# C's projection in the output projection's banks, the third token form two weight units sooner, v scaled by quarters

## The chip, the cores and the metric

The kernel runs on one NeuronCore of a Trainium2 chip. The metric is the device time of one execution in microseconds, as the median of several. Its engines have a queue each and work in the order of their queues: TensorE (PE, with its weight loads as PEld), VectorE (DVE), ScalarE (ACT), GpSimd (POOL) and SyncE (SP, which issues most of the DMAs).

## What is computed

Two layers over 640 tokens (512 of a new stream and 8 x 16 of running streams) with 1024 channels, and a final norm. Layer A is a Mamba-2 mixer, layer B a gated MLP whose positions are mixed:

```python
# layer A, per group of 4 heads (8 groups)
xbc_c = silu(causal_dwconv(xbc, conv_prev, conv_w, conv_b))   # x (2 tiles of 128), B, C
y, ssm_new = ssd_scan(xs, dt, a, bm, cm, ssm_prev)            # C B^T, decay, states
y = gated_group_rms_norm(y + d_skip * xs, z, norm_w)
h = h + y @ w_out
# layer B
u = gelu(proj[..., :2048]); v = gelu(proj[..., 2048:4096]); z = proj[..., 4096:]
v = layer_norm(v, ln_w, ln_b)
s = einsum('gts,bksgc->bktgc', wm, vc) + b_sp                 # positions mixed, 8 groups
h = h + (u * s * silu(z)) @ w_out
```

All products run as three products of high and low parts (`hi*hi + lo*hi + hi*lo`), so weights and tokens are split into two tiles (`wh`, `wl` or `wf`, and `xH`, `xL`).

## The kernel before

**Layer A** goes through 8 groups. A group projects x0, x1, B, C, z0 and z1 (`in_proj`: two token halves of 384 and 256, 8 steps each, 16 in all; a step is three matmuls per 128 rows of weights). Work of other kinds is put between these steps: `side` is a list of closures, and `in_proj` takes one from it (`pump`) after each step named in `at`. `queue(j)` (L521) puts two closures there, which transpose the convolved tile j (0 and 1 are x0 and x1, 2 is B) to tokens: four tiles, then one (L472, tile `tp`, in ps_y). `conv_tile` reads a projection's two banks on VectorE (L415 to L417) and convolves it (L422, L425, L431, L432). After that a group runs its scan: `prompt_states` (tile `st` in ps_op, read by L569 into `hs`), `old_states` (`yq` in ps_op, read by L585), `cb_prompt` and `cb_sample` (ps_m), the masks (L634: the decays E of four heads times CBm, three on VectorE and one on GpSimd) and two pairs of heads (`yA`, `yB`, both in ps_y). In groups 1 to 6 the output projection of the group before is mixed in as ten pieces (`some`, L610): a piece is six matmuls into a bank named by the letter at its place in a string (o is ps_op, y is ps_y, m is ps_m), and is drained by L689 on VectorE. The order is: states 0, piece 0, old states, C B^T, piece 1, states 1, pieces 2 to 4, first mask, first pair, second mask, pieces 5 to 9, second pair.

PSUM has four pools of two banks: ps_in, ps_m, ps_y and ps_op. x0, x1, C, z0 and z1 are projected in ps_in, and B in ps_m. In layer A the order of TensorE is the order of the program; the order of the other engines and queues is set by Tile's scheduler, which works by priority and a model of its own.

**Layer B** has the order of all engines written by hand. First `v_tiles` makes v in four blocks of 512 columns (`vb`), tile by tile of 128 tokens (the last two tiles, 3 and 4, together), in four weight units u of 256 rows; after each unit it calls `unit(u)`. GELU is L844, the statistics L847. In the last block `unit` fills the first weight forms of the next stage: `forms.fill(2 * u + 2)`; a form is a 512-column combination of weight blocks, split by a cast on ScalarE (L751) and a subtraction on VectorE (L752), with L763, L765, L766 and L770 for the combinations. Forms of the tokens are made too: `t1_` to `t4_` between the tiles; the third, `t3`, is written over block (0, 1) of xH and xL by `hilo` (L905 on ScalarE, L906 on VectorE) after the last block, for that block is still read by the v matmuls. `t3` lies in a pool (`tfp`) that is closed there, and the tiles of the next stage (`wkb`: rsb, c1, uu, zz) take its memory.

Then 16 steps f (two per group g) compute u and z by seven products of 320 columns (Strassen-Winograd), in the order m1, m6, m5, m2, m7, m3, m4, in the banks pa, pb and pc. Between them stand c1 (L1015 reads pa), L1018 (reads pb), L1022 (reads pc), GELU (L1025, L1036), L1030, L1035 and L1049; m2 overwrites pa after L1015, m7 goes on in pb after L1018, m3 in pc after L1022, m4 in pb after L1030. `prod` first fills the weight forms five ahead. `v_norm(t)` (L850) scales v[:, t] to the layer norm: statistics and rsqrt on VectorE, then two activations of 1024 columns (L859); tiles 0 to 2 in the v stage, tiles 3 and 4 in step f = 0, behind L1025 and behind L1030. v's quarter f // 4 is read by the position mix of step f. Gating work of a step is put off into `later`, of which `then()` takes one entry between the products of the next step, and `then(9)` all that are left. In steps 3, 5, ..., 13 the ten output pieces of the group before come first, each drained by L968.

The lines that the change touches: L528 and L531 (the projections of B and C in groups 1 to 7), L610 (the banks of the pieces), L850 to L859 (`v_norm`), L946 and L947 (`unit` and `hilo`), L1027, L1032 and L1081 (`v_norm(3)`, `v_norm(4)` and `later`).

Of the kernel before, what the change touches and what calls it, by code (L numbers as in the profile page):

```python
# [8 lines left out]
F32 = mybir.dt.float32  # L9
F32R = mybir.dt.float32r  # L10
I32 = mybir.dt.int32
AF = mybir.ActivationFunctionType
# [3 lines left out]
P = 128  # L16
D = 1024
NT = 640
TT = 5
# [21 lines left out]
def hybrid_step(ctx: ExitStack, tc: tile.TileContext, xin, xT0, cst, wdt, cache, wA, wAo, h0in, wB, wBv, wBo,  # L41
                lnwb, spc, bsp, nwb, y_out, nconv_out, sspP_out, sspS_out, v_out):
    nc = tc.nc
    V, S, G, T = nc.vector, nc.scalar, nc.gpsimd, nc.tensor
# [217 lines left out]
    def in_proj(W, xT, pool=None, tag="in", at=(1, 3, 5, 7, 9, 11, 13)):  # L262
        outs = []
        for h, (a, b) in enumerate(HALVES):
            o = (pool or ps_in).tile([P, 512], F32, name="pin", tag=tag)[:, :b - a]
            outs.append(o)
            for k in range(KD):
                in_proj_step(W, xT, o, h, k)
                if 8 * h + k in at:
                    pump()  # L270
        return outs


    def out_proj(Ws, ys, acc, pieces=range(2 * TT), banks="oyoyoyoyoy", after=None, at=(1, 3)):
        for p in pieces:
            t, dh = p // 2, p % 2
            tsl = slice(t * P, (t + 1) * P)
            dsl = slice(dh * 512, (dh + 1) * 512)
            ps = bank(banks[p], "pop")
            n = len(ys)  # L280
            for i in range(n):
                (wH, wL), (yH, yL) = Ws[i], ys[i]
                mm(ps, yH[:, tsl], wH[:, dsl], start=(i == 0), stop=False)
                mm(ps, yL[:, tsl], wH[:, dsl], start=False, stop=False)
                mm(ps, yH[:, tsl], wL[:, dsl], start=False, stop=(i == n - 1))
            acc(ps, t, dsl)
            if after is not None:
                after(t, dsl, dh)
            if p in at:
                pump()  # L290
# [33 lines left out]
    with ExitStack() as ca:  # L324
# [123 lines left out]
        for g in range(GROUPS):  # L448
# [76 lines left out]

            if g:
                queue(0, *(() if g == 1 else (0,)))
                o = in_proj(stream.next(), xT, ps_m, "m", at=(3, 7, 11, 14))  # L528
                xcs.append(conv_tile(*o, 16 + g, 2, *cio))
                queue(1, *(() if g == 1 else (1,)))  # L530
                o = in_proj(stream.next(), xT, at=(3, 7, 11, 14))  # L531
                xcs.append(conv_tile(*o, 24 + g, 3, *cio))
                queue(2, *((0, 1, 2, 3) if g == 1 else (2, 3)))
            else:
                queue(0, 0)
                queue(1, 1)
                queue(2, 2, 3)
# [69 lines left out]
            ssd = [lambda: prompt_states(0), old_states, cb_prompt, lambda: prompt_states(1), cb_sample]  # L607
            if 0 < g < GROUPS - 1:
                Wo = [stream.next(), stream.next()]
                some = lambda a, b: out_proj(Wo, *pend[g - 1], range(a, b), "yyomoooyoo")  # L610
                ssd[0]()
                some(0, 1)
                ssd[1]()
                ssd[2]()
                some(1, 2)
                ssd[3]()
                ssd[4]()
                some(2, 5)
            elif last:
                side.extend(ssd)  # L620
                zrs.append(gate_in((1, 3, 5, 7, 9, 11, 13)))
                pump(9)
            else:
                side.extend(ssd)
                xin1 = in_proj(stream.next(), xT, at=(1, 3, 5, 8, 10))
                pump(9)
                cio1 = conv_io(1)
# [163 lines left out]
    with ExitStack() as cb_:  # L791
# [58 lines left out]
        def v_norm(t):  # L850
            mv = small.tile([P, 2], F32, name="mv")
            V.bn_aggr(out=mv, in_=st6[:, t])
            rs = rsqrt(mv[:, 1:2], EPS, 1)
            nm = small.tile([P, 1], F32, name="nm")
            V.scalar_tensor_tensor(nm, mv[:, 0:1], -1.0, rs, ALU.mult, ALU.mult)
            vt = v[:, t].rearrange("p a b -> p (a b)")
            for q in range(2):
                qs = slice(q * 1024, q * 1024 + 1024)
                S.activation(vt[:, qs], vt[:, qs], AF.Identity, scale=rs, bias=nm)  # L859

        def position(g):

# [32 lines left out]
        with tc.tile_pool(name="tfp", bufs=1) as tfp:  # L895
            ta, tb, t3, tx = [tfp.tile([P, 4, HT], F32, name=f"tx{i}") for i in range(4)]

            def sub(out, a, b):
                V.tensor_tensor(out=out, in0=a, in1=b, op=ALU.subtract)

            def add(out, a, b):
                V.tensor_tensor(out=out, in0=a, in1=b, op=ALU.add)

            def hilo(t, H, L):
                S.copy(out=H, in_=t)  # L905
                V.tensor_tensor(out=L, in0=t, in1=H.bitcast(F32), op=ALU.subtract)  # L906

            f11, f12, f21, f22 = [[x.bitcast(F32) for x in block(k, j)] for k in range(2) for j in range(2)]

            def t1_():  # L910
                sub(ta, f12[0], f11[0])
                sub(tx, f12[1], f11[1])
                add(ta, ta, tx)
                hilo(ta, tf[:, 0, 0], tf[:, 0, 1])

            def t2_():
                sub(tb, f22[0], ta)
                add(tb, tb, f22[1])
                hilo(tb, tf[:, 1, 0], tf[:, 1, 1])

            def t4_():
                sub(ta, f21[0], tb)
                add(ta, ta, f21[1])
                hilo(ta, tf[:, 2, 0], tf[:, 2, 1])

            def t3_():
                sub(t3, f22[0], f12[0])
                sub(tx, f22[1], f12[1])
                add(t3, t3, tx)

            between = {(1, 0): t1_, (1, 1): t2_, (2, 0): t4_, (2, 1): t3_}
            for vb in range(1, 4):
                W, vsp = vsp, []
                if vb < 3:
                    for u in range(4):
                        v_fetch(4 * vb + 4 + u)
                else:
                    forms.fetch()
                    forms.fetch()
                    pos = position(0)  # L940
                for t in range(3):
                    v_tiles(W, vb, (t,))
                    between.get((vb, t), lambda: None)()
                    if vb == 3:
                        v_norm(t)
                v_tiles(W, vb, (3, 4), unit=(lambda u: v_split()) if vb < 3 else (lambda u: forms.fill(2 * u + 2)))  # L946
            hilo(t3, *block(0, 1))  # L947
        wk = cb_.enter_context(tc.tile_pool(name="wkb", bufs=2))

        X = dict(m1=block(0, 0), m2=block(1, 0), m3=block(1, 1), m7=block(0, 1))  # L950
# [38 lines left out]
        for g in range(GROUPS):  # L989
# [9 lines left out]
            for i in range(2):  # L999
# [24 lines left out]
                prod(pa, "m2", False)  # L1024
                S.activation(uu[:, lo], pa, AF.Gelu)  # L1025
                if f == 0:
                    v_norm(3)  # L1027
                then()
                prod(pb, "m7", False)
                V.tensor_tensor(out=zz[:, hi], in0=pb, in1=c5, op=ALU.add)  # L1030
                if f == 0:
                    v_norm(4)  # L1032
                then(9)
                prod(pc, "m3", False)
                V.tensor_tensor(out=uu[:, hi], in0=pc, in1=uu[:, hi], op=ALU.add)  # L1035
# [42 lines left out]

                if f:
                    positions()  # L1080
                    later.extend([gate1, gate2, new_v])  # L1081
                else:
                    later.extend([gate1, lambda m=mix, p=positions: (m(), p()), gate2, new_v])

# [133 lines left out]
```

## Time and profile before

| | |
|---|---|
| median of 3 runs | 1084.14 us (1083.35 to 1085.52) |
| the profiled execution | 1084.73 us |
| its span, first to last instruction | 1083.0 us |
| mean granted TensorE clock | 0.983 |
| layer A | about 0 to 597 us |
| the v stage of layer B | about 597 to 718.6 us |
| the 16 steps and the end | 718.6 to 1083 us |

The profile is one execution. Starts and durations are in microseconds from the span's start. TensorE matmuls are pipelined, so their durations overlap. In brackets behind a row of the timeline stands how long the engine was idle before it, and what ended that.

### The profile page before, as it was taken

How to read it: one execution, taken by the hardware profiler on the slowest of the kernel's cores; microseconds unless marked ns; L12 is line 12 of the kernel's file. 1: busy time of each engine (PE TensorE's matmuls, PEld its weight loads, DVE VectorE, ACT ScalarE, POOL GpSimd, SP SyncE). 2: the span in 40 equal slices, each digit the busy share in tenths (PEclk: the TensorE clock that was granted, in tenths of full speed). 3: DMA queues.
4: the chain of work that ended last, by engine and by line, in shares of the span. 5: the costliest groups of instructions: out<-in, count | busy, mean ns of one | idle time of the engine just before them, and what ended most of it. 6: DMA issues, size and time to landing. Idle time of an engine off the chain costs nothing.

```text
span 1083.0 us, 16928 instructions
## 1 busy us (share of the span) xinstructions
PE 1032.2 (95%) x6387; PEld 932.8 (86%) x6387; DVE 862.7 (80%) x1608; ACT 470.2 (43%) x917; POOL 127.0 (12%) x172
## 2 busy tenths in 40 slices
PE   8997999999999999999999899977999999999996
PEld 7987889899798898998987678867998998988984
DVE  7767797878978878788889756566889888889876
ACT  6464617338264282552732433344333333333343
POOL 1022221302213022021130000000000000000000
PEclk9899899999999999999999999999999999999999
DMA  6574638457285473753624122211323322412322
GB/s 243 157 204 129 191 90 244 109 180 175 86 249 124 150 193 97 231 136 118 192 71 171 50 78 78 88 51 49 98 76 90 117 59 86 138 54 90 91 69 97
DMA packets 59808, 135.37 MB, mean 125 GB/s; under 512 B 9392, under 2 KB 28080, under 8 KB 59728
## 3 DMA queue, kind: packets, MB, share of 16 engines
q1 hardware_dynamic: 56848, 123.82, 36.1%
q0 software_dynamic: 2880, 10.49, 5.8%
q8 instruction: 50, 0.82, 0.3%
q14 instruction: 30, 0.25, 0.1%
HBM read 117.42 MB, written 16.86 MB: 124 GB/s over the span
## 4 chain that ended last, share of the span: by engine, by line
PE 62%; DVE 20%; ACT 5%; issue 3%; DMA 2%; SPq 0%; ACTq 0%; DVEq 0%
PE pin L69 26%; PE pop L69 11%; PE pv L69 9%; DVE wf L752 3%; PE pqb L69 3%; PE pqa L69 2%; PE pqc L69 2%; PE st L69 2%; DVE h L968 2%; PE yB L69 2%; DVE uu L1063 1%; PE tp L472 1%; DVE thb L1062 1%; DVE uu L1066 1%; ACT wf L751 1%
## 5 line engine op out<-in xcount | busy, mean ns | idle before, releaser
L69 PE MATMUL pin<-xH,wh 128*128 128x384 f32 (+1 forms) x768 | 249.4, 325 | 2.6 <-DVE xp L413 1.9
L69 PE MATMUL pin<-xH,wl 128*128 128x384 f32 (+1 forms) x768 | 239.6, 312 | 0.0
L69 PE MATMUL pin<-xL,wh 128*128 128x384 f32 (+1 forms) x768 | 239.5, 312 | 0.0
L69 PEld LDWEIGHTS pin<-xH,wh 128*128 128x128 f32 x768 | 147.6, 192 | 9.9 <-issue 4.1
L69 PEld LDWEIGHTS pin<-xL,wh 128*128 128x128 f32 x768 | 147.7, 192 | 0.4 <-issue 0.3
L69 PEld LDWEIGHTS pin<-xH,wl 128*128 128x128 f32 x768 | 147.3, 192 | 0.2 <-DVE wl L104 0.2
L425 DVE SCALAR_TENSOR_TENSOR acc<-xp,cw,acc 128x664 f32<-128x664 f32 x96 | 94.7, 987 | 30.7 <-ACT acc L422 29.5
L69 PE MATMUL pop<-wf,yHL 128*128 128x512 f32 x480 | 115.2, 397 | 1.4 <-DVE h L968 0.7
L69 PEld LDWEIGHTS pop<-wf,yHL 128*128 128x128 f32 x480 | 89.2, 188 | 25.4 <-DVE h L968 3.6
L752 DVE TENSOR_TENSOR wf<-raw,wf 128x512 fp32r<-128x512 f32 x128 | 86.6, 686 | 29.4 <-ACT wf L751 28.3
L99 ACT CAST wh<-raw 128x1024 fp32r<-128x1024 f32 x63 | 65.7, 1043 | 100.7 <-PE pin L69 62.6
L69 PE MATMUL pop<-wh,yHL 128*128 128x512 f32 x320 | 103.3, 404 | 5.1 <-DVE hs L569 4.7
L751 ACT CAST wf<-raw 128x512 fp32r<-128x512 f32 x128 | 76.5, 617 | 53.9 <-PE pop L69 27.2
L69 PEld LDWEIGHTS pop<-wh,yHL 128*128 128x128 f32 x320 | 57.8, 188 | 20.5 <-DVE hs L569 6.9
L69 PE MATMUL pqa<-xH,wf 128*128 128x320 f32 x256 | 64.3, 320 | 7.2 <-ACT c L1015 7.2
L689 DVE SCALAR_TENSOR_TENSOR h<-pop,rr,h 128x512 f32<-128x512 f32 x80 | 58.9, 744 | 12.1 <-PE pop L69 11.9
L69 PE MATMUL pv<-wh,xL 128*128 128x512 f32 x160 | 63.0, 394 | 2.4 <-DVE xL L235 2.4
L69 PE MATMUL pv<-wh,xH 128*128 128x512 f32 x160 | 63.4, 396 | 0.9 <-DVE xL L235 0.8
L69 PE MATMUL pqb<-tf,wf 128*128 128x320 f32 x384 | 63.0, 313 | 1.0 <-DVE zz L1030 1.0
L69 PE MATMUL pv<-wl,xH 128*128 128x512 f32 x160 | 63.0, 394 | 0.0
L69 PE MATMUL pop<-wl,yHL 128*128 128x512 f32 x160 | 62.6, 391 | 0.0
L104 DVE TENSOR_TENSOR wl<-raw,wh 128x1024 fp32r<-128x1024 f32 x43 | 53.6, 1245 | 9.2 <-ACT wh L99 9.1
(223 smaller groups left out, 1966.3 us busy)
## 6 DMA issues: line engine op xcount, KB each, us to landing
raw<-wA SPq DMA_DIRECT2D x47, 512.0 KB, 3.8
raw<-wB SPq DMA_DIRECT2D x32, 512.0 KB, 4.0
E<-laD SPq DMA_DIRECT2D x32, 320.0 KB, 5.8
h<-h0in SPq DMA_DIRECT2D x16, 512.0 KB, 5.0
raw<-wAo SPq DMA_DIRECT2D x16, 512.0 KB, 4.8
out_sspS<-h SPq DMA_DIRECT2D x16, 512.0 KB, 3.7
raw<-wBv SPq DMA_DIRECT2D x16, 512.0 KB, 4.4
raw<-wBo SPq DMA_DIRECT2D x16, 512.0 KB, 3.8
```

The source lines that it names most:

```text
L69: T.matmul(out, lhsT=lhsT, rhs=rhs, start=start, stop=stop, **kw)
L99: S.copy(out=H, in_=raw)
L104: V.tensor_tensor(out=L, in0=raw, in1=H.bitcast(F32), op=ALU.subtract)
L425: V.scalar_tensor_tensor(acc[:, 0:664], xp[:, k:k + 664], cw[:, 4 * ft + k:4 * ft + k + 1], acc[:, 0:664], ALU.mult, ALU.add)
L472: T.transpose(out=tp[:, t - ta, :], in_=xcs[j][:, t * P:(t + 1) * P], identity=ident)
L689: V.scalar_tensor_tensor(h1[:, t, dsl], ps, rg[:, t:t + 1], h1[:, t, dsl], ALU.mult, ALU.add)
L751: S.copy(out=t[:, 0], in_=src)
L752: V.tensor_tensor(out=t[:, 1], in0=src, in1=t[:, 0].bitcast(F32), op=ALU.subtract)
L968: V.scalar_tensor_tensor(h1[:, t, dsl], ps, 0.5, h1[:, t, dsl], ALU.mult, ALU.add)
L1062: V.scalar_tensor_tensor(th, th, 1.0, zz, ALU.add, ALU.mult)
L1063: V.tensor_tensor(out=uu, in0=uu, in1=th, op=ALU.mult)
L1066: V.tensor_tensor(out=uu, in0=uu, in1=sb.rearrange("p a b -> p (a b)"), op=ALU.mult)
```

## The change

There are three edits. In groups 1 to 7 of layer A, C is projected in ps_op instead of ps_in, B's projection takes its side work after steps 5, 9, 12 and 14 instead of 3, 7, 11 and 14, and piece 2 of the output projection uses ps_y instead of ps_op. In layer B, `hilo` of t3 is issued after unit 1 of the last v tiles, between `fill(4)` and `fill(6)`, instead of behind the whole block. And `v_norm` of tiles 3 and 4 scales the first 512 columns at once, by a copy of the factor (`rq`, so that it outlives the rotating tile of rsqrt); the other three quarters of both tiles go into `later`, two in each of steps 1, 2 and 3, to be run in the step after.

```diff
@@ -525,10 +525,10 @@
             if g:
                 queue(0, *(() if g == 1 else (0,)))
-                o = in_proj(stream.next(), xT, ps_m, "m", at=(3, 7, 11, 14))
+                o = in_proj(stream.next(), xT, ps_m, "m", at=(5, 9, 12, 14))
                 xcs.append(conv_tile(*o, 16 + g, 2, *cio))
                 queue(1, *(() if g == 1 else (1,)))
-                o = in_proj(stream.next(), xT, at=(3, 7, 11, 14))
+                o = in_proj(stream.next(), xT, ps_op, "op", at=(3, 7, 11, 14))
@@ -607,7 +607,7 @@
-                some = lambda a, b: out_proj(Wo, *pend[g - 1], range(a, b), "yyomoooyoo")
+                some = lambda a, b: out_proj(Wo, *pend[g - 1], range(a, b), "yyymoooyoo")
@@ -851,12 +851,22 @@
-            nm = small.tile([P, 1], F32, name="nm")
+            nm = small.tile([P, 1], F32, name="nm", bufs=TT)
             V.scalar_tensor_tensor(nm, mv[:, 0:1], -1.0, rs, ALU.mult, ALU.mult)
-            vt = v[:, t].rearrange("p a b -> p (a b)")
-            for q in range(2):
-                qs = slice(q * 1024, q * 1024 + 1024)
-                S.activation(vt[:, qs], vt[:, qs], AF.Identity, scale=rs, bias=nm)
+            if t > 2:
+                rq = small.tile([P, 1], F32, name="rq", bufs=2)
+                V.tensor_copy(rq, rs)
+
+            def scale(qs, r=rs if t < 3 else rq):
+                vt = v[:, t].rearrange("p a b -> p (a b)")
+                S.activation(vt[:, qs], vt[:, qs], AF.Identity, scale=r, bias=nm)
+
+            if t < 3:
+                for q in range(2):
+                    scale(slice(q * 1024, q * 1024 + 1024))
+                return []
+            scale(slice(0, 512))
+            return [lambda q=q: scale(slice(q * 512, q * 512 + 512)) for q in range(1, 4)]
@@ -943,8 +953,13 @@
-                v_tiles(W, vb, (3, 4), unit=(lambda u: v_split()) if vb < 3 else (lambda u: forms.fill(2 * u + 2)))
-            hilo(t3, *block(0, 1))
+
+                def last_units(u):
+                    forms.fill(2 * u + 2)
+                    if u == 1:
+                        hilo(t3, *block(0, 1))
+
+                v_tiles(W, vb, (3, 4), unit=(lambda u: v_split()) if vb < 3 else last_units)
@@ -1024,12 +1039,12 @@
                 if f == 0:
-                    v_norm(3)
+                    rest = v_norm(3)
...
                 if f == 0:
-                    v_norm(4)
+                    rest = [x for p in zip(rest, v_norm(4)) for x in p]
@@ -1078,7 +1093,7 @@
-                    later.extend([gate1, gate2, new_v])
+                    later.extend([gate1, gate2, new_v] + (rest[2 * f - 2:2 * f] if f < 4 else []))
```

## Rows read from the trace of the kernel before

**Rows 1.** The page, part 1: engine, busy us, share, instructions.
```profile
PE 1032.2 (95%) x6387; PEld 932.8 (86%) x6387; DVE 862.7 (80%) x1608; ACT 470.2 (43%) x917; POOL 127.0 (12%) x172
```
**Rows 2.** Timeline of TensorE, group 1 (start, duration, engine, line, operation, [idle before]).
```profile
108.27 1.09 PE L472 MATMUL tp<-csb,xc 128*128 128x128 f32 x4 [4.38 <-DVE y L655]
125.00 0.41 PE L69 MATMUL pin<-xH,wh 128*128 128x384 f32 x1 [1.87 <-DVE xp L413]
```
**Rows 3.** Waits of TensorE, whole span: waiter, releaser, total us, times, longest.
```profile
PE pop L69 <- DVE hs L569: 4.7, 5, 1.0
```
**Rows 4.** Windows: stretch, length, busy us by engine, clock, DMA share, GB/s.
```profile
718.60:762.40 43.80, 31.79 (x192) 30.23 (x191) 31.30 (x67) 19.41 (x33) 1.08 (x3) 0.92 0.21 62
```
**Rows 5.** Timeline of TensorE, group 3: piece 4 and the first pair's yB.
```profile
352.72 0.73 PE L69 MATMUL pop<-wh,yHL 128*128 128x512 f32 x2 [0.94 <-DVE hs L569]
...
354.21 0.83 PE L69 MATMUL yB<-xc,hs 128*128 128x128 f32 x6
```
**Rows 6.** Timeline of VectorE, group 3: masks and the drain of piece 2.
```profile
350.15 2.18 DVE L634 TENSOR_TENSOR E<-E,CBm 128x640 f32<-128x640 f32 x1
...
352.59 0.74 DVE L689 SCALAR_TENSOR_TENSOR h<-pop,rr,h 128x512 f32<-128x512 f32 x1
353.25 0.81 DVE L634 TENSOR_TENSOR E<-E,CBm 128x640 f32<-128x640 f32 x1
```
**Rows 7.** Timeline of GpSimd, group 3.
```profile
349.91 1.74 POOL L634 TENSOR_TENSOR E<-E,CBm 128x640 f32<-128x640 f32 x1
```
**Rows 8.** Timeline, group 1: B's convolved tile on VectorE, its transposes on TensorE.
```profile
125.08 0.90 DVE L432 SCALAR_TENSOR_TENSOR xc<-xc,acc 128x512 f32<-128x512 f32 x2 [0.22 <-ACT xc L431]
...
127.74 1.06 PE L472 MATMUL tp<-csb,xc 128*128 128x128 f32 x4
```
**Rows 9.** Timeline of TensorE, steps f = 0 and f = 3.
```profile
730.00 0.63 PE L69 MATMUL pqa<-xH,wf 128*128 128x320 f32 x1 [5.54 <-ACT c L1015]
...
786.15 5.86 PE L69 MATMUL pop<-wf,yHL 128*128 128x512 f32 x24 [0.30 <-DVE h L968]
```
**Rows 10.** Timeline of ScalarE, end of the v stage and step f = 0.
```profile
723.72 1.27 ACT L905 CAST xH<-tx 128x1280 fp32r<-128x1280 f32 x1
729.24 0.37 ACT L996 COPY rsb<-pr 128x256 f32<-128x256 f32 x1 [4.25 <-DVE xL L906]
...
740.10 2.38 ACT L859 ACTIVATE v<-v,nm,rr 128x1024 f32<-128x1024 f32 x2 [3.44 <-DVE nm L855]
742.38 0.60 ACT L751 CAST wf<-raw 128x512 fp32r<-128x512 f32 x1
```
**Rows 11.** Timeline of VectorE, end of the v stage and step f = 0.
```profile
720.42 0.69 DVE L770 TENSOR_TENSOR raw<-raw 128x512 f32<-128x512 f32 x1
...
723.34 0.69 DVE L752 TENSOR_TENSOR wf<-raw,wf 128x512 fp32r<-128x512 f32 x1 [0.80 <-ACT wf L751]
...
727.68 1.47 DVE L906 TENSOR_TENSOR xL<-tx,xH 128x1280 fp32r<-128x1280 f32 x1
729.98 0.49 DVE L1018 TENSOR_TENSOR uu<-pqb,c 128x320 f32<-128x320 f32 x1 [0.82 <-ACT c L1015]
...
737.30 0.48 DVE L1030 TENSOR_TENSOR zz<-pqb,c 128x320 f32<-128x320 f32 x1
...
746.50 0.48 DVE L1049 TENSOR_TENSOR zz<-pqb,c 128x320 f32<-128x320 f32 x1
```
**Rows 12.** Groups by line and shape: times, busy us, mean ns; one line's durations.
```profile
L859 ACT ACTIVATE v<-v,nm,rr 128x1024 f32<-128x1024 f32 x10 | 11.9, 1236 | 12.9 <-DVE nm L855 12.9
L751 ACT CAST wf<-raw 128x512 fp32r<-128x512 f32 x128 | 76.5, 617 | 53.9 <-PE pop L69 27.2 <-DVE raw L766 23.3 <-PE pv L69 2.1
L823 ACT CAST wh<-raw 128x1024 fp32r<-128x1024 f32 x16 | 16.7, 1048 | 23.6 <-PE pv L69 13.3 <-DMA raw<-wBv 8.9 <-issue 1.4
L200 DVE COPY rs<-rr x1: 171/171/171, 29.0 to 29.0; 128x5 f32<-128x5 f32 x1
```
**Rows 13.** The chain of waits at f = 5's pieces: start, us, what.
```profile
827.89 2.13 PE pop L69 x8
```

## The prediction

> **What bounds the kernel now.** I read the engine lines of the page first: TensorE is busy for 1032.2 of 1083.0 us [rows 1], so a change is worth only what it takes out of the remaining 51 us. Next I listed every wait of TensorE over 0.1 us in the timeline. Apart from start-up, the passage between the layers (580 to 625 us) and the tail, they stand where the change works. In layer A, group 1 has one wait of 4.38 us ahead of x0's transposes and one of 1.87 us at the start of z0's projection [rows 2]; groups 2 to 6 have one each, 4.7 us for five, all on the last update of hs (L569) [rows 3]. At the start of layer B, TensorE works 31.79 of the 43.80 us from 718.6 to 762.4 [rows 4]: that is the largest hole that the change can reach. There VectorE and ScalarE, in the order written by hand, are behind, and TensorE follows them.
>
> **Bank change, groups 2 to 6.** The output projection's piece 4 ("o") sits 0.94 us behind the L569 that reads the second st tile [rows 5]: ps_op has two banks, piece 2 took the one that yq had left, so piece 4 gets the bank of st. With piece 2 in "y", piece 4 gets yq's bank, and yq was read by about 346, before piece 2 began. That wait of 0.94 us goes, five times 4.7 us at most. What is late next: ps_y has two banks too, and pieces 0, 1, 2 and then yA, yB of the first pair go through them. One of yA, yB now follows piece 2, whose drain is the L689 at 352.59, ending 353.33 [rows 6]. TensorE would come to yB (which runs first) at 354.21 - 0.94 = 353.27 [rows 5], so it waits for that drain and 0.06 us of hand-over (as much as lies between L569 and piece 4), to 353.39. The pair's second mask (L634 at 353.25) ends at 354.06 [rows 6], before the product that reads it, about 1 us into yB. That makes 0.82 us won at best; since mask and drain each end within 0.2 us of their use, I take 0.7, 5 x 0.7 = **3.5 us**. The ends are 5 x 0.1 = 0.5 (yB behind a drain that comes after the second mask too) and 4.7 (a drain in time). Below nothing is possible only if the scheduler, which orders VectorE, ScalarE, GpSimd and the queue here by its own model, moves that drain back (rival 3).
>
> The drain is late because the first mask takes 2.18 us where the second takes 0.81 [rows 6]; GpSimd runs its own mask from 349.91 to 351.65 meanwhile [rows 7]. The Trainium skill (SBUF — State Buffer, section Who interferes with whom) says that a VectorE instruction with two SBUF inputs and a GpSimd instruction that reads SBUF block each other for a whole instruction, by issue order. The rows fit that: 351.65 + 0.7 is the mask's end. By that rule a scheduler that put the drain ahead of the mask would lose nothing on the mask; it is rival 2.
>
> **Bank change, group 1.** z0's projection waits 1.87 us because it reuses C's bank in ps_in, still unread by the convolution (L415) [rows 2]. With C in ps_op, z0's first bank is that of x1, read 25 us earlier; the wait goes. C's own banks in ps_op are wanted next by st, a whole z0 projection (about 7 us) later, so that step costs nothing; without that cover it would cost the same 1.87 us. B's pumps move from steps 3 and 7 to 5 and 9: the x0 transposes that wait 4.38 us for VectorE's L655 get two steps of six matmuls ahead of them. Six matmuls at one per 0.17 us (the full clock just before) are 1.04 us, which fill part of the wait. Together 2.9 us is free. But z0's own pump after step 2 transposes B's convolved tile, and that comes from VectorE (L432) at 125.98 [rows 8], whatever TensorE does. Before, those transposes ran at 127.74 [rows 8]; now they can run from 126.0. So **1.8 us** (0 if the scheduler delays that convolution, 2.9 if it comes sooner). In the other groups x0's transposes are not waited for; moving them back 1.04 us is hidden by the 15 us of projections ahead of st.
>
> **Third form (hilo of t3) earlier.** TensorE's longest wait, 5.54 us ahead of the fourth product, is on c1 (L1015) [rows 9]. ScalarE reached the copy before it, rsb, long before, but rsb lies in memory freed by t3 and stood 4.25 us behind L906 [rows 10], the last op of the form on VectorE (727.68, 1.47 us) [rows 11]. Placed after fill(4), the cast L905 (1.27 us) follows that unit's two casts, so it is done near 720.7, and L906 follows L770 (720.42 + 0.69) at once, ending about 722.5 [rows 10, 11]. Its inputs are free: it overwrites rows 0 to 3 of the blocks, which the matmuls of units 0 and 1 read until about 713. Units 2 and 3 read rows 4 to 7, so nothing new waits. rsb and c1 then follow ScalarE's own work, near 724.6, and the fourth product can start about 5 us sooner. The gain is less than that, for the fifth product accumulates on a bank that VectorE must read first (L1018). VectorE's work up to L1018 is the same in the other order; only its idle time goes: 0.80 us at 723.34 and 0.82 at 729.98 [rows 11], 1.62 us, and some tenths inside merged rows. I take **1.7 us** (1.0 if one wait comes back on another cast, 5.5 as the upper end).
>
> **Scaling v by quarters.** Each v_norm holds ScalarE for two halves, from 740.10 to the next cast at 742.38, 2.28 us [rows 10]; that cast feeds the wf op that stands ahead of L1030 or L1035 on VectorE, so all of VectorE waits (L1030 at 737.30, L1049 at 746.50) [rows 11]. A quarter: a half takes 1236 ns, a cast of 1024 columns 1048, of 512 columns 617 [rows 12], so 1236 - 431 = 805 ns, and 0.71 us to the next start (halves overlap by 0.1). Saved 2.28 - 0.71 = 1.57 us, less the new copy rq (171 ns for a copy of five columns [rows 12], 0.19 with its gap) ahead of the scaling: 1.38 us, two tiles **2.76 us** (2.2 if the quarter costs the full 0.81 plus a longer copy; 3.3 if it costs a plain cast's 0.53). The chain from L1030 to the end of f = 1 is VectorE without a hole, so this reaches TensorE in full.
>
> The six other quarters go into the queue of later steps in f = 2, 3 and 4, two each, 0.71 us apiece on ScalarE. In f = 2 they stand ahead of the casts for L1030's and L1035's products; the wf ops of these have a few tenths of slack, so VectorE slips about 0.5 us, and it is the bound there: the pieces wait 0.30 us for it at 786.15 [rows 9]. In f = 3 ScalarE idles and TensorE leads: nothing. In f = 4 the chain goes straight from VectorE's L968 into the pieces of f = 5 at 827.89 [rows 13], no slack, 0.5 again. **-1.0 us** (0 if the slack is larger, -2.8 if four quarters count in full). DMAs and queues: no step that issues one moves.
>
> **Sum.** 1.8 + 3.5 + 1.7 + 2.76 - 1.0 = 8.8 us. The profiled execution took 1084.73 us (span 1083.0), 0.59 above the median 1084.14; against the median the forecast is 1084.1 - 8.8 = **1075.3**, say 1075.4.
>
> **Rivals.**
> 1. Layer A gives nothing: the wait at piece 4 comes back at yB or at the mask, and group 1 is held by its convolutions. For it: VectorE has hardly a hole from 348 to 357. Against it: rows 6 put the drain's end 0.9 us ahead of yB's old start. Only layer B's 1.7 + 2.76 - 1.0 = 3.5 is left: 1080.6. If also the deferred quarters count nearly in full (-2.8 instead of -1.0), 1082.4, within the 0.2%.
> 2. More: the scheduler puts the drain of piece 2 ahead of the mask, which is blocked anyway until 351.65, so yB waits for nothing (4.7 in place of 3.5), and group 1 gives 2.9 in place of 1.8: 2.3 us more, 1073.0.
> 3. Slower: the same drain is put behind the masks and the next drains. yB, and all of the group behind it, starts when L689 ends. Each of groups 2 to 6 then loses what the drain's end is past 354.2, its start now. With 1.8 + 3.5 won elsewhere, it turns slower by over 2.2 us when that is more than 1.5 us per group, a drain ending past 355.7; behind the two other masks and one further drain, three ops of 0.7 to 0.8 us more [rows 6], it ends near 355.6. At 2 us the time is 1084.1 - 5.3 + 10 = 1088.8. Against it: the drain is ready before those ops.
> 4. It doesn't do what it says: the bank handed to piece 4 is again that of st, and rsb still waits for another tile of the closed pool. Then only the quarters act, 2.76 - 1.0: 1082.4.
>
> **How the numbers follow.** Forecast (1073.7 to 1079) 0.58; rival 1 0.18 (a third of it within 0.2%); rival 2 0.12; rival 3 0.06; rival 4 0.06. The range leaves out rival 3, rival 4 and the low end of rival 2: 1071.0 to 1081.5; the upper end is rival 1 with half of the extra loss. About 0.2% (2.2 us) is what a measurement of this kernel tells from no change: faster 0.84, same 0.11, slower 0.05.
>
> **What would show it.** Right: no TensorE wait on L569 in groups 2 to 6; none at z0 in group 1, but a new one of 2 to 3 us at B's transposes; L905 and L906 done before 723 and rsb without a wait; L1018 near 728; L1049 of f = 0 near 742. Wrong: waits of TensorE on L689 ahead of yB of about the old 0.94; L1018 still near 730; new waits of over 0.5 us at the pieces of f = 3 or 5.

## The result and the profile after

The changed kernel takes 1072.75 us (median of 4 runs, 1071.28 to 1074.0), the kernel before 1084.27 beside it: ratio 0.9892, 95% interval 0.9874 to 0.991, or 11.5 us less. The forecast was 1075.4 in a range of 1071.0 to 1081.5. The profiled execution took 1072.77 us, its span is 1071.0.

In the page's first part TensorE is busy for 7 us less than before [rows 1], for the same 6387 products. That is not 7 us of gain: the mean granted clock of this execution is 0.989 instead of 0.983, and a second profile of the changed kernel has 1028.2 us of busy time at 0.986 in a span of 1071.1. How much of the gain shows as busy time and how much as idle time depends on the execution.

```profile
PE 1025.1 (96%) x6387; PEld 927.4 (87%) x6387; DVE 859.8 (80%) x1610; ACT 470.4 (44%) x921; POOL 128.5 (12%) x172
```

The same stretch as [rows 4], from pr of step 0 to pr of step 2 (pr is the small product that opens every second step), in the windows view (length, busy us of PE, PEld, DVE, ACT and POOL, clock, DMA share, GB/s): it is 38.57 us long, where it was 43.8. The granted clock is 1.00 here, where it was 0.92, but the second profile of the changed kernel has 38.59 us at 0.96, so the clock is not what made this stretch shorter.

```profile
712.24:750.81 38.57, 29.12 (x191) 27.33 (x190) 31.31 (x69) 15.84 (x30) 1.63 (x4) 1.00 0.23 74
```

TensorE after, in the timeline. First group 1, to be read against [rows 2] and [rows 8]: the wait of x0's transposes is shorter, z0's wait has gone, and B's transposes wait instead. Then group 3 at piece 4, against [rows 5]: the pieces follow each other without a hole, and so does yB. Then steps 0, 1 and 3, against [rows 9]: the wait of 5.54 us has gone, and step 0 has two of about 2 us instead. The last two rows are waits that stood there before: the one on L1037 in step 1 was 2.40 us (on L1022), and the one at the pieces of step 3 was 0.30.

```profile
106.12 1.09 PE L472 MATMUL tp<-csb,xc 128*128 128x128 f32 x4 [3.30 <-DVE y L655]
...
124.05 0.63 PE L472 MATMUL tp<-csb,xc 128*128 128x128 f32 x4 [2.59 <-DVE xc L432]
...
347.57 0.40 PE L69 MATMUL pop<-wl,yHL 128*128 128x512 f32 x1
347.81 0.63 PE L69 MATMUL pop<-wh,yHL 128*128 128x512 f32 x2
348.28 0.39 PE L69 MATMUL pop<-wl,yHL 128*128 128x512 f32 x1
348.51 0.83 PE L69 MATMUL yB<-xc,hs 128*128 128x128 f32 x6
...
722.16 0.41 PE L69 MATMUL pqb<-xH,wf 128*128 128x320 f32 x1 [1.98 <-DVE uu L1033]
...
727.97 2.03 PE L69 MATMUL pqb<-tf,wf 128*128 128x320 f32 x12 [2.03 <-DVE zz L1045]
...
744.85 0.41 PE L69 MATMUL pqc<-xH,wf 128*128 128x320 f32 x1 [2.42 <-DVE c L1037]
...
774.99 5.75 PE L69 MATMUL pop<-wf,yHL 128*128 128x512 f32 x24 [0.72 <-DVE h L983]
```

ScalarE after, against [rows 10]: the form's cast (L915) stands among the weight casts, rsb follows without a wait, and a quarter of v takes 0.81 us where two halves took 2.38.

```profile
713.06 1.26 ACT L915 CAST xH<-tx 128x1280 fp32r<-128x1280 f32 x1
...
717.37 0.38 ACT L1011 COPY rsb<-pr 128x256 f32<-128x256 f32 x1
...
725.47 0.81 ACT L862 ACTIVATE v<-v,nm,rq 128x512 f32<-128x512 f32 x1 [3.97 <-DVE rq L858]
726.19 0.60 ACT L751 CAST wf<-s 128x512 fp32r<-128x512 f32 x1
```

VectorE after, against [rows 11]: the form's subtraction (L916) is done at 716.2, L1033 (L1018 before) runs 8.4 us earlier, L1064 (L1049 before) 11.2 us earlier (6.3 us of each is the lead that pr of step 0 has already). What still waits for a quarter is the wf operation behind a cast that stands behind it, 1.39 us, twice. Behind quarters that were put off VectorE waits 0.16 us (shown) and 0.14 in step 2, and 0.17 and 0.14 in step 4.

```profile
714.69 1.49 DVE L916 TENSOR_TENSOR xL<-tx,xH 128x1280 fp32r<-128x1280 f32 x1
...
721.63 0.47 DVE L1033 TENSOR_TENSOR uu<-pqb,c 128x320 f32<-128x320 f32 x1
...
726.83 0.69 DVE L752 TENSOR_TENSOR wf<-s,wf 128x512 fp32r<-128x512 f32 x1 [1.39 <-ACT wf L751]
...
735.27 0.48 DVE L1064 TENSOR_TENSOR zz<-pqb,c 128x320 f32<-128x320 f32 x1
...
761.88 0.69 DVE L752 TENSOR_TENSOR wf<-raw,wf 128x512 fp32r<-128x512 f32 x1 [0.16 <-ACT wf L751]
```

To find where the time went, I set the starts of the same TensorE operations of two traces beside each other. Three distances serve below: a group of layer A (the mean over groups 2 to 5, from one group's first yq, the product of `old_states`, to the next group's), steps 0 and 1 (pr of step 0 to pr of step 2), and steps 4 to 13 (pr of step 4 to pr of step 14).

| kernel | a group | steps 0, 1 | steps 4 to 13 | median | ratio to before, 95% |
|---|---|---|---|---|---|
| before, two profiles | 69.47, 69.47 | 43.81, 43.97 | 208.69, 208.84 | 1084.27 | |
| after, two profiles | 68.58, 68.65 | 38.57, 38.59 | 208.08, 207.78 | 1072.75, 1073.01 | 0.9892 and 0.9906 |
| e1_bank | 68.36 | 43.92 | 208.29 | 1076.42 | 0.9943 (0.9923 to 0.9963) |
| e2_form | 69.46 | 41.44 | 208.89 | 1082.51 | 0.9994 (0.9977 to 1.001) |
| e3_quarters | 69.75 | 41.40 | 207.92 | 1082.83 | 0.9998 (0.9984 to 1.0012) |
| g1_shift | 69.69 | 43.93 | 207.86 | 1085.53 | 1.0018 (1.0005 to 1.003) |
| g2_unshift | 68.38 | 38.62 | 208.65 | 1072.36 | 0.9901 (0.9882 to 0.9919) |
| h1_string | 68.59 | 38.60 | 207.92 | 1075.77 | 0.9933 (0.9918 to 0.9948) |
| g4_stats | 68.38 | 34.60 | 208.97 | 1068.73 | 0.9864 (0.9843 to 0.9886) |
| h2_fill | 68.41 | 32.51 | 209.16 | 1067.60 | 0.9856 (0.9841 to 0.9871) |
| h3_pad | 68.43 | 34.65 | 208.23 | 1069.46 | 0.9871 (0.9855 to 0.9886) |
| h4_all | 68.43 | 32.49 | 208.20 | 1065.29 | 0.9831 (0.9812 to 0.985) |

### The profile page after: what moved, and what is told of

Read it like the earlier page. It is cut to its first block, busy times and chain, and to the rows that moved or that the text cites. A ratio compares the mean times of both kernels' runs of the same rounds, so it can differ in the third digit from the quotient of the medians.

```text
span 1071.0 us, 16927 instructions
## 1 busy us (share of the span) xinstructions
PE 1025.1 (96%) x6387; PEld 927.4 (87%) x6387; DVE 859.8 (80%) x1610; ACT 470.4 (44%) x921; POOL 128.5 (12%) x172
## 4 chain that ended last, share of the span: by engine, by line
PE 62%; DVE 19%; ACT 5%; issue 3%; DMA 1%; SPq 0%; ACTq 0%; DVEq 0%
PE pin L69 25%; PE pop L69 13%; PE pv L69 10%; PE pqb L69 3%; DVE wf L752 3%; PE pqc L69 2%; PE pqa L69 2%; DVE h L983 2%; PE st L69 2%; PE yB L69 1%; ACT wf L751 1%; DMA E<-laD 1%; DVE uu L1078 1%; DVE thb L1077 1%; DVE uu L1081 1%
## 5 line engine op out<-in xcount | busy, mean ns | idle before, releaser
L69 PE MATMUL pop<-wf,yHL 128*128 128x512 f32 x480 | 112.6, 392 | 3.2 <-DVE h L983 2.7
L425 DVE SCALAR_TENSOR_TENSOR acc<-xp,cw,acc 128x664 f32<-128x664 f32 x96 | 90.7, 944 | 28.5 <-ACT acc L422 27.3
```

The costliest lines, as they stand in the source:

```text
L69: T.matmul(out, lhsT=lhsT, rhs=rhs, start=start, stop=stop, **kw)
L425: V.scalar_tensor_tensor(acc[:, 0:664], xp[:, k:k + 664], cw[:, 4 * ft + k:4 * ft + k + 1], acc[:, 0:664], ALU.mult, ALU.add)
```

## The experiments

### The kernel before once more

No edit.

> The kernel before once more, unchanged, for a second profile of it. If the start-up differs from one execution to the next, this profile's marks at 45 us and in the passage at 580 to 625 us differ from the first profile's by up to 2.5 us although nothing is changed, and the granted clock of 10 to 30 us differs too; its time stays within 1 us of 1084.1. If they lie within 0.3 us of the first profile, the 2.3 us by which the changed kernel is ahead at 45 us come from the edit.

It took 1083.99 us, ratio 1.0013 (0.9997 to 1.0028) to the same program beside it. The marks differ although nothing was changed: its yq of group 1 comes 3.07 us earlier than in the first profile, and the way from the last pss of layer A (the sums for a group's norm) to pr of step 0 is 1.0 us longer. The windows view of group 1 and of the passage between the layers, first the first profile, then this one, shows why:

```profile
110.00:140.00 30.00, 28.13 (x187) 25.98 (x187) 23.08 (x56) 18.30 (x44) 8.15 (x9) 0.92 0.61 170
580.00:600.00 20.00, 18.31 (x89) 14.24 (x87) 18.48 (x46) 5.28 (x9) 0.00 (x0) 1.00 0.59 212
```

```profile
110.00:140.00 30.00, 28.86 (x199) 26.27 (x199) 24.88 (x61) 18.00 (x44) 11.21 (x14) 0.99 0.63 166
580.00:600.00 20.00, 16.32 (x79) 12.36 (x77) 17.98 (x48) 7.08 (x10) 0.00 (x0) 0.97 0.54 186
```

The granted clock was 0.92 and 1.00 in one execution, 0.99 and 0.97 in the other. The changed kernel's first trace was 2.3 us ahead of the first of before at 45 us (43.21 instead of 45.51); this second profile of before is at 46.55 there, and the second profile of the changed kernel (below) at 45.50. So that lead is a matter of the execution, and stretches before 180 us and between 580 and 625 us can't be priced from one pair of profiles. The three distances of the table repeat within 0.2 us.

### The first edit alone

```diff
-  o = in_proj(stream.next(), xT, ps_m, "m", at=(3, 7, 11, 14))
+  o = in_proj(stream.next(), xT, ps_m, "m", at=(5, 9, 12, 14))
-  o = in_proj(stream.next(), xT, at=(3, 7, 11, 14))
+  o = in_proj(stream.next(), xT, ps_op, "op", at=(3, 7, 11, 14))
-  "yyomoooyoo"
+  "yyymoooyoo"
```

> The first edit alone (C in ps_op, B's later pumps, piece 2 in ps_y); layer B as in the kernel before. Theory (the terms add, and the pieces give their whole wait): groups 2 to 6 give 0.9 us each, 4.5 us, and group 1 gives 0.5 us net, because what it wins ahead of yq is taken back before its end: 5.0 us faster than before, near 1079.2. Rival (the numbers as predicted): 3.5 + 1.8 = 5.3 us, so the total can't tell these two apart and the shift of yq and of pss in group 1 has to. Second rival (layer A's gain seen in the trace of the changed kernel is partly another execution's start-up): no more than 3 us faster, near 1081. In the trace the start-up (up to 45 us), which no edit touches, stands within 0.3 us of the trace of before if the 2.3 us seen there come from the edit, and anywhere within some 2.5 us if it is a matter of the single execution.

6.3 us faster (1082.71 beside it), more than any of the three expected, though 5.0 and 5.3 lie within its interval (4.0 to 8.3). A group takes 68.36 instead of 69.47 us: 1.11 us less, not 0.9. The timeline of TensorE at piece 4 in the second profile of before shows what that is:

```profile
348.44 0.62 PE L69 MATMUL pop<-wh,yHL 128*128 128x512 f32 x2
348.90 0.39 PE L69 MATMUL pop<-wl,yHL 128*128 128x512 f32 x1
350.23 0.73 PE L69 MATMUL pop<-wh,yHL 128*128 128x512 f32 x2 [0.94 <-DVE hs L569]
```

From the last product of piece 3 to the first of piece 4 are 1.33 us, and without a wait they are 0.23 (347.78 to 348.01 in the next rows). The wait cost 1.10 us; the 0.94 in brackets is counted from the modelled end of a product that overlaps its successor by 0.16. The other half is yB. TensorE and VectorE of this kernel in group 3:

```profile
347.78 0.39 PE L69 MATMUL pop<-wl,yHL 128*128 128x512 f32 x1
348.01 0.61 PE L69 MATMUL pop<-wh,yHL 128*128 128x512 f32 x2
348.46 0.39 PE L69 MATMUL pop<-wl,yHL 128*128 128x512 f32 x1
348.69 0.83 PE L69 MATMUL yB<-xc,hs 128*128 128x128 f32 x6
```

```profile
345.86 2.18 DVE L634 TENSOR_TENSOR E<-E,CBm 128x640 f32<-128x640 f32 x1
347.97 0.41 DVE L569 TENSOR_TENSOR hs<-st,hs 128x256 f32<-128x256 f32 x1
348.30 0.73 DVE L689 SCALAR_TENSOR_TENSOR h<-pop,rr,h 128x512 f32<-128x512 f32 x1
348.96 0.81 DVE L634 TENSOR_TENSOR E<-E,CBm 128x640 f32<-128x640 f32 x1
```

Piece 2's drain ends at 349.03, and yB started at 348.69: it didn't wait for that drain, so its bank is the one that piece 1 left; piece 2's falls to yA, which comes over a microsecond later. The mask of 2.18 us is as long as before; by the Trainium skill's rule (SBUF — State Buffer, Who interferes with whom) it would be, and the trace agrees, but nothing on the path stands behind it any more.

### The second and the third edit alone

```diff
   forms.fill(2 * u + 2)
+  if u == 1:
+      hilo(t3, *block(0, 1))
...
-  hilo(t3, *block(0, 1))
```

> The second edit alone: the third token form after unit 1 of the last two v tiles; layer A and the scaling of v as before. Theory (VectorE bounds the passage into the 16 steps, so only its idle time is won): 1.6 to 1.9 us faster, 1082.4, and L1018 of f = 0 about 1.7 us nearer to the start of the step. Rival (the wait of 5.54 us for c1 was the bound, VectorE's queue has holes that the page merges): 2.5 to 3.5 us faster, near 1081.2. Second rival (the scaling in halves takes the gain back, because ScalarE then holds VectorE's wf operation a little later on): under 1 us.

```diff
-  for q in range(2): S.activation(half q of v[:, t])
+  rq = copy of rs;  scale(slice(0, 512))
+  return [the other three quarters]      # into later, two a step
```

> The third edit alone: v's tiles 3 and 4 scaled by quarters, six quarters put off into f = 2 to 4; the form and layer A as before. Theory (the terms add): 2.76 us won in f = 0, 0.3 us given back by the quarters put off, so 2.4 us faster, 1081.7. Rival (as predicted, 1.0 us given back): 1.8 us, 1082.4. Second rival (the form and the quarters fall on the same chain, so that each alone gives less than its part of the 5.2 us that both gave): under 1.5 us faster, and the two alone sum to 3.5 us or less.

Both edits are shown in short. By the times neither edit can be told from no change. In the trace steps 0 and 1 are 2.45 us shorter with the form (43.9, the mean of before, to 41.44) and 2.5 us shorter with the quarters (to 41.40); both together gave 5.3 (to 38.58). VectorE of the second edit alone, at the two casts behind the scaling in halves, and of the third alone:

```profile
728.99 0.47 DVE L1023 TENSOR_TENSOR uu<-pqb,c 128x320 f32<-128x320 f32 x1
...
735.69 0.69 DVE L752 TENSOR_TENSOR wf<-s,wf 128x512 fp32r<-128x512 f32 x1 [2.95 <-ACT wf L751]
```

```profile
739.40 0.69 DVE L752 TENSOR_TENSOR wf<-s,wf 128x512 fp32r<-128x512 f32 x1 [1.47 <-ACT wf L751]
740.73 0.49 DVE L1040 TENSOR_TENSOR zz<-pqb,c 128x320 f32<-128x320 f32 x1 [0.64 <-PE pqb L69]
```

With the form alone, L1023 stands 9.39 us behind pr of step 0 (719.6), in the kernel before 11.40 (729.98 and 718.58): 2.0 us. With the quarters alone, each wait of 2.95 us becomes 1.4 to 1.5, but now VectorE waits 0.64 us for TensorE, whose fourth product still starts late because of the form. In the changed kernel that wait isn't there: the two edits help each other, by 0.4 us in steps 0 and 1.

The third edit also changes a group of layer A, 69.75 us instead of 69.47, where no line of it was touched. What it does change there is the place of the tiles: nm's ring is one tile longer and rq has two, 32 bytes each, so every tile allocated behind them lies 96 bytes further on. The next section shows what that costs; in this run it takes back most of the 2.5 us.

### The place of the tiles

```diff
# g1_shift: the kernel before
-  nm = small.tile([P, 1], F32, name="nm")
+  nm = small.tile([P, 1], F32, name="nm", bufs=7)
# g2_unshift: the changed kernel
-  ss = small.tile([P, 1], F32, name="ss")
+  ss = small.tile([P, 1], F32, name="ss", bufs=1)
```

> The kernel before with nothing but nm's ring made seven tiles long, which puts every tile allocated behind it 96 bytes further on in SBUF, as the third edit does by nm's fifth tile and rq's two. Theory (the place of the tiles sets the pace of the products): groups 2 to 6 take 69.69 us each instead of 69.48, yq to yq, as in the third edit alone, so 1.5 us slower in all, 1084.4 beside 1082.9 for before. Rival (the third edit's copy and quarters, or that one execution, made the groups longer): 69.48 us a group and no difference.

> The changed kernel with the 96 bytes taken off elsewhere (the ring of ss, used once, made one tile long), so that every tile of layers A and B lies where it lay before the change. Theory (the place of the tiles): groups 2 to 6 take 68.36 us each as in the first edit alone, not 68.57, and the whole is 1.3 to 1.5 us faster than the changed kernel on the same chip. Rival (the place doesn't matter): 68.57 us a group and the time of the changed kernel within 0.5 us.

> The changed kernel again, unchanged, beside the others of this call and with a second profile. Theory: its start-up and its group 1 differ from the first profile's by up to 3 us, because TensorE's clock falls at other moments of the first 140 us in each execution, and the passage between the layers by up to 1 us; groups 2 to 6 take 68.57 us each again and the stretch from pr of f = 0 to pr of f = 2 38.6 us again, within 0.1 us. 10 to 11.5 us faster than before. Rival (start-up and passage belong to the program): they repeat within 0.3 us.

A group takes 69.69 us with the shift alone and 68.38 when the changed kernel's shift is taken back, where its own two profiles have 68.58 and 68.65: 0.2 us a group. From yq of group 2 to the last pss of layer A it is 377.4 us without the shift (both profiles of before) and 378.7 with it, 1.3 us. But steps 4 to 13 go the other way: 207.9 with the shift, 208.7 and 208.8 without. In the view of groups by line and shape (times, busy us, mean ns, idle before), the output pieces alone change their pace (all others stay within 2 ns). Layer A's, in groups 2 to 6, for the second profile of before and for the shift alone:

```profile
L69 PE MATMUL pin<-xH,wl 128*128 128x256 f32 x184 | 51.9, 282 | 0.0
L69 PE MATMUL pop<-wl,yHL 128*128 128x512 f32 x76 | 29.7, 391 | 0.0
```

```profile
L69 PE MATMUL pin<-xH,wl 128*128 128x256 f32 x184 | 51.9, 282 | 0.0
L69 PE MATMUL pop<-wl,yHL 128*128 128x512 f32 x78 | 31.0, 397 | 0.0
```

Layer B's, from 805 to 1000 us, for the kernel before and for the changed kernel:

```profile
L69 PE MATMUL pop<-wf,yHL 128*128 128x512 f32 x298 | 71.7, 397 | 0.7 <-DVE h L968 0.4
```

```profile
L69 PE MATMUL pop<-wf,yHL 128*128 128x512 f32 x300 | 70.5, 392 | 2.0 <-DVE h L983 2.0
```

The projections (pin) have 282 ns in both. The ends of products are modelled, but the starts say the same: from one product of a piece to the next it is 229.5 ns in the old place and 233.8 with the shift in layer A, 233.5 and 227.8 in layer B. Of the pieces' operands it is yHL that was moved, not the weights. 6 ns more in layer A, 5 ns fewer in layer B, whose yHL tiles lie elsewhere; and the faster pieces of layer B then wait longer for their drains (L983), so not all of it is kept. Why 96 bytes do this no run here shows.

Group 1, which these distances leave out, has a cost of its own. VectorE there, first in the kernel before, then with the shift alone:

```profile
142.20 0.42 DVE L568 TENSOR_TENSOR hs<-hs,etot 128x256 f32<-128x256 f32 x1
142.53 1.24 DVE L634 TENSOR_TENSOR E<-E,CBm 128x640 f32<-128x640 f32 x1
```

```profile
140.35 0.90 DVE L568 TENSOR_TENSOR hs<-hs,etot 128x256 f32<-128x256 f32 x1
141.17 2.19 DVE L634 TENSOR_TENSOR E<-E,CBm 128x640 f32<-128x640 f32 x1
```

Counted from the group's first yq, L568 starts 0.03 us later with the shift, beside a multiplication of GpSimd (L590). In the old place L568 took 0.42 us and that L590 0.85; now L568 takes 0.90 and L590 0.61, the mask behind it takes 2.19 us instead of 1.24, and TensorE waits 0.95 us for L569 ahead of piece 4. By the starts that is 1.1 us. The three profiles with the old letter in group 1 and the shift (e3_quarters, g1_shift, h1_string) have this wait, the three with the old letter and the old place (both of before, e2_form) don't. Since the slower pieces stand just ahead of it, I take them for the cause of the 0.03 us; no run shows that by itself.

In time the shift alone costs 2.0 us (0.5 to 3.2 by the interval), the traces 1.3 + 1.1 - 0.8 = 1.6. The third edit alone has the same costs: in its trace 2.5 us won in steps 0 and 1 and 0.85 in steps 4 to 13 stand against 1.5 lost in groups 2 to 6, 1.1 in group 1 and 0.2 in steps 2 and 3, so about 0.5 us are left of the gain. Taking the shift out of the changed kernel, where piece 4 of group 1 waits for nothing, gave 0.65 us between medians, less than the 1.3 to 1.5 expected; by the traces layer B's gain goes with it. The repeated changed kernel repeats the three distances within 0.3 us. Its start-up doesn't repeat: the mark at 45 us comes 2.3 us later than in the first profile, yq of group 0 0.7 and yq of group 1 0.5 us later.

### Group 1

```diff
-  C in ps_op, B's pumps at (5, 9, 12, 14)
+  C in ps_in, B's pumps at (3, 7, 11, 14), as before the change
-  "yyymoooyoo"
+  "yyomoooyoo" if g == 1 else "yyymoooyoo"
```

> The changed kernel with C in ps_in and B's pumps at 3, 7, 11, 14 again, and piece 2 in ps_y in groups 2 to 6 alone: of the first edit only the letter is left, and group 1 is as before the change. Theory (the letter makes the gain of groups 2 to 6, C's banks and the pumps serve group 1 alone, where most of what they win is given back): 68.57 us a group, yq to yq, in groups 2 to 6, as in the changed kernel; in group 1 the wait of 1 to 3 us at z0's projection is back; 0.5 us slower than the changed kernel, 1073.4. Rival (group 1 gives the 1.8 us of the prediction): 1.8 us slower, 1074.7. Second rival (C's banks matter in groups 2 to 6 too): 69.0 us a group or more, and over 2.5 us slower.

A group takes 68.59 us, as in the changed kernel: the gain of groups 2 to 6 is the letter's alone. In group 1 the old waits are back, and with them the one of 0.95 us at piece 4 that comes with the shift and that neither profile of before has:

```profile
106.93 1.08 PE L472 MATMUL tp<-csb,xc 128*128 128x128 f32 x4 [4.30 <-DVE y L655]
...
122.80 0.41 PE L69 MATMUL pin<-xH,wh 128*128 128x384 f32 x1 [1.13 <-DVE xp L413]
...
141.87 0.73 PE L69 MATMUL pop<-wh,yHL 128*128 128x512 f32 x2 [0.95 <-DVE hs L569]
```

In time it is slower than the changed kernel by 0.0027 of before, 2.9 us, with an uncertainty of 2.5 (the two intervals' half-widths, 0.0015 and 0.0018, added as squares). But 1.1 us of that is the wait at piece 4, which the kernel before hasn't, so 1.8 us with the same uncertainty are left for C's banks and the pumps: neither the prediction's 1.8 nor my 0.5, which I had from one pair of traces, is excluded. The profiles don't settle it either. From yq of group 0 to yq of group 2 it is 126.96 us here and 126.83 and 127.06 in the changed kernel; over all fourteen profiles it is 127.6 on average in the three with the old group 1 and the old place (125.4 to 130.0) and 126.2 in the eight with the new group 1 (124.7 to 127.1). The difference of 1.4 us lies within the scatter of the three.

### Two steps further

If VectorE's queue is what holds steps 0 and 1, taking work and waits out of it must go on paying. g4_stats computes the statistics of both tiles in one chain behind L1045 and scales the first quarters behind the next product's cast; h2_fill adds the second edit shown; h3_pad adds the third to g4_stats; h4_all has all. The edits are shortened.

```diff
# g4_stats (with the tiles in their old place)
-  rest = v_norm(3)                          # behind L1040
-  rest = zip(rest, v_norm(4))               # behind L1045
+  rest = v_norm2()                          # behind L1045: one rsqrt of two columns, no rq
   prod(pc, "m3", False)
+  rest.pop(0)(); rest.pop(0)()              # the first quarters
# h2_fill, for f < 2, ahead of the GELU of uu[:, hi] and ahead of the tanh
+  forms.fill(6)
# h3_pad, ahead of v
+  bp.tile([P, 24], F32, name="pad")
```

> The changed kernel with the statistics of v's tiles 3 and 4 taken together behind L1045 (one chain of small operations instead of two, no copy rq), their first quarters scaled behind the cast that the next product needs, and the tiles in their old place. Theory (VectorE's queue is still the bound from f = 0 to f = 2): its two waits of 1.39 us for a cast behind the scaling go, and some 2 us of small operations; 3.5 to 4.5 us less from pr of f = 0 to pr of f = 2 (34.5 us instead of 38.6), and with 1.4 us from the place of the tiles about 5.5 us faster than the changed kernel. Rival (TensorE's products or ScalarE's copy c bound it there already): under 1.5 us less in that stretch, 2.5 us in all.

> The kernel with the common statistics (g4_stats), and in steps 0 and 1 the next product's weight cast put ahead of the GELU and the tanh in ScalarE's order. Theory (VectorE's remaining waits for such a cast, 1.05, 1.31 and 1.05 us, still hold TensorE up): they go, and TensorE follows by 2.0 to 2.4 us from pr of f = 0 to pr of f = 2 (32.4 us instead of 34.6), 1066.5 in all. Rival (TensorE's own products are the bound from f = 1 on): under 0.8 us, 1068.

> The kernel with the common statistics (g4_stats), with an unused tile of 96 bytes ahead of v in layer B's pool: layer A's tiles lie as before the change, layer B's as after it. Theory (the place of layer B's own tiles sets the pace of its steps): layer A as in g4_stats (68.36 us a group), and 0.6 to 0.8 us less from pr of f = 4 to pr of f = 14, as in the changed kernel and in the kernel with only the shift: 208.25 us there instead of 208.97; 1068.0 in all. Rival (the 0.7 us of the later steps come from another cause): 208.97 us and 1068.7.

> The last two together: casts ahead of GELU and tanh in steps 0 and 1, and the 96 bytes ahead of v. Theory (the terms add): 32.4 us from pr of f = 0 to pr of f = 2, 208.25 from f = 4 to f = 14, 1065.8 in all, 7 us faster than the changed kernel. Rival (what is won by f = 2 is given back at the output pieces of f = 3 and 5, which wait for VectorE): 1067 or more.

g4_stats shortens steps 0 and 1 by 4.0 us, h2_fill by another 2.1, both as their theory had it. In time g4_stats is 4.3 us faster than the changed kernel beside it (1073.01), not 5.5: the old place was put at 1.4 us and gives about 0.5 by the traces. Between h2_fill and g4_stats, timed in different series, the ratios give less than the times can tell. Of TensorE's waits of over 0.25 us in that stretch g4_stats has two, h4_all three, and one more at the pieces of step 3:

```profile
721.26 0.41 PE L69 MATMUL pqb<-xH,wf 128*128 128x320 f32 x1 [1.99 <-DVE uu L1036]
...
739.65 0.42 PE L69 MATMUL pqc<-xH,wf 128*128 128x320 f32 x1 [2.42 <-DVE c L1040]
```

```profile
720.50 0.42 PE L69 MATMUL pqb<-xH,wf 128*128 128x320 f32 x1 [1.99 <-DVE uu L1037]
...
737.11 0.41 PE L69 MATMUL pqc<-xH,wf 128*128 128x320 f32 x1 [1.15 <-DVE c L1041]
741.24 2.00 PE L69 MATMUL pqb<-tf,wf 128*128 128x320 f32 x12 [0.98 <-DVE zz L1047]
...
766.36 5.73 PE L69 MATMUL pop<-wf,yHL 128*128 128x512 f32 x24 [0.95 <-DVE h L987]
```

The 96 bytes in layer B alone give their 0.7 us from step 4 to 14 in the traces (208.97 to 208.23), but h3_pad's median is 0.7 us above that of g4_stats, which was timed in another series: less than the times can tell. h4_all takes 1065.29 us, 1.7% less than the kernel before beside it, and 7.5 us less than the changed kernel, which was timed in another series (6.6 and 8.1 us by the ratios to before). The rival for it is half there: the pieces of step 3 wait 0.95 us now.

## Why the prediction came out

The direction and the range held. The parts, by the forecast's own terms:

- **Groups 2 to 6: 3.5 us expected.** The letter gave 5 x 1.1 = 5.5, and the shift of the tiles took back 1.3 in layer A. Two steps were wrong, both to the safe side. The wait was priced by the 0.94 us in brackets, and its cost is the distance of the starts, 1.10. And yB was put behind piece 2's drain, but that bank went to yA. No wait on L569 is left, as forecast.
- **Group 1: 1.8 expected.** The waits did as forecast: none at z0, and a new one at B's transposes. Its 2.59 us lie in the forecast's "2 to 3 us" by luck: the second profile of the same kernel has 1.16, and those of the other kernels with the new group 1 have from under 0.25 to 3.15. What group 1 gave is not settled (above).
- **Form: 1.7 expected, 2.0 measured** at VectorE's L1023, and 2.45 by step 2. The 1.62 us of idle time was right as a floor. L905 and L906 done before 723, rsb without a wait, L1018 near 728: in the changed kernel, with its lead of 6.34 us at pr of step 0 added, L1033 stands at 727.97.
- **Quarters: 2.76 expected.** VectorE's two waits went from 2.95 to 1.39 us each, 3.12, less two copies of 0.08 (L855 to L858): 2.96. A quarter took 0.80 to 0.82 us; 805 ns was forecast. The Trainium skill (ScalarE: Activation LUTs, What ACT_TABLE_LOAD costs) gives 186 ns, 93 for each of two pointer operands and 0.833 a column, an estimate of 799: the trace agrees. L1049 of step 0, with the same lead added, stands at 741.6; near 742 was forecast.
- **Quarters put off: -1.0 expected.** In steps 2 and 4 VectorE waits 0.3 us each for casts behind them, where 0.5 each was forecast, and in step 3 nothing, as forecast. The forecast named waits of over 0.5 us at the pieces of steps 3 and 5 as a sign that it was wrong, and they came (0.72 and 0.59). Several edits have a share in them: the kernel before has 0.30 and 0.14 there, the shift alone 0.50 and 0.29, the changed kernel with its tiles in the old place (g2_unshift) 0.62 and 0.38. Steps 2 and 3 together are 0.3 us longer than before, but 0.5 longer with the form alone, where no quarter is put off. So the term was too large; how much of it there is no run separates.
- **Not foreseen:** the 96 bytes, -1.3 us in groups 2 to 6 and +0.8 in layer B. The 1.1 us in group 1 come with the old letter only, so the changed kernel doesn't pay them.

Sum of what the distances show: 5.5 - 1.3 + 0.8 + 5.3 = 10.3 us, less 0.3 in steps 2 and 3 (43.15 instead of 42.85), plus group 1: 10 us and something for group 1, against 9.7 (the medians of the second series) and 11.5 (of the first). The forecast of 8.8 was low for groups 2 to 6, the form and the quarters, and high for the quarters put off, and it left out the shift, whose two parts partly cancel: that the total came so near is in part luck, while the mechanism of each edit is seen in the rows. Rival 2 (1073.0) came nearest in time, by another way: nothing was reordered on VectorE, and the drain of piece 2 stands where the forecast had it. Rivals 1, 3 and 4 are refuted by the same rows.

## What to carry to other kernels

Price a wait of TensorE by the distance between two starts with and without it, not by the idle time printed behind the row. Where two edits serve one queue, time them together too: alone each gave 2.5 us of the 5.3 in the traces, which times that scatter by 2 us, and a side effect as large as the gain, didn't show. And an edit that adds a few small tiles moves all tiles behind them, which here changed the pace of products and brought a wait of 1.1 us into one group: keep the place of the others when parts are compared.

## What the runs showed that was not expected

A shift of 96 bytes in SBUF changes products whose stationary operand (yHL) was moved, from 391 to 397 ns a product in layer A and from 397 to 392 in layer B, with none of the others changed by more than 2 ns (pin 282 in both); the seven profiles with the old place in layer B and the seven with the new one have 208.8 us (208.3 to 209.2) and 208.0 (207.8 to 208.2) on average for steps 4 to 13. The cause is open. And the granted clock of one program differs between executions, where TensorE waits in the first 140 us and between the layers: 0.92 and 0.99 in the same 30 us of two executions, and 3 us between the marks behind them.
